# Attention plan on measured durations, weights on ScalarE's transfer queue, low parts in quarters, a reordered front

## The chip, the cores and the metric

One NeuronCore of a Trainium2 chip runs the program. The metric is the device time in microseconds (us) of one execution. Below, PE is TensorE, ACT is ScalarE, DVE is VectorE, POOL is GpSimd and SP is SyncE; "ACTq" and "SPq" are the places on ACT and SP where transfers are issued.

## What is computed

A hybrid encoder block in float32 on 512 tokens of 1024 channels, with 16 learned meta tokens in front (528 columns in all):

```python
u = rms_norm(h, pre_mix_gain);  proj = u @ w_in
qa, ka, va, qb, kb, vb, g = split(proj)
qa, ka, qb, kb = rope(...)                 # on each
o_swa  = windowed_gqa_sink_attention(qa, ka, va, sink)      # 16 q heads, 4 kv heads, blocks of 128
o_diff = rms_norm((softmax(q1 k1) - lam * softmax(q2 k2)) @ vb) * (1 - lambda_init)   # 8 heads
merged = sigmoid(g1) * (o_swa @ w_branch_swa) + sigmoid(g2) * (o_diff @ w_branch_diff)
h = h + rms_norm(merged @ w_out)
f = (silu(u2 @ w_gate) * (u2 @ w_up)) @ w_ffn_out;  h = h + rms_norm(f)     # u2 = rms_norm(h), 2816 wide
```

## The kernel before

Each float32 operand is split into a high part and a low part (`wh`, `wl`; `xh`, `xl`), and each product is three matmuls: high by high, high by low, low by high (`mm3`, lines 287 to 289). The weights come in tiles of 128 x 1024 (512 KB). For each one, `weights` (line 520) issues the transfer into `wr` (L527, on SP; three buffers), casts the high part on ACT (L529) and subtracts the low part on POOL for odd tiles and on DVE for even ones (L253). `products` (line 536) makes eight k-steps of `mm3` from one tile; each waits for all of `wh` and `wl`.

The program has four parts. In the **front**, 60 small matmuls on zeros (`warm`, L380) run first. Then the K projection (L447) takes its two weight tiles in parts of 2, 2 and 4 k-steps, the V projections follow (`pV`, then `pV2` by `v2(0)` and `v2(1)`), and between them the row sums of squares give the normalizing factors `rbc` (L491, L492). The order here is the order of the text.

The **attention plan** comes next. `Plan` holds a list of tasks with an engine, a cost, what they read and write, buffers with slots, and a priority. `Plan.run` walks through time: for each engine it finds the tasks that can start first and takes the one that is due first (for PE the priority itself, for the others the time at which it could start plus a slack by priority). Tasks with `port` never overlap each other. The engines then run in just this order; on the chip every wait is a semaphore, so a wrong cost changes the order and not the result. The tasks are: V for the windowed heads (`v_swa`), the rotated K (`rope_t`, L554 to L558, then transfers between partitions by `move`, L576), four groups of Q (`q_swa`), gates (`gate`), 16 windowed units (`s_swa`: scores `Sw` L715, exponentials, scaling on POOL L729; `t_swa`: transposes L764, products `O` L771), then per differential head `qk`, `vd`, `s_diff` (scores `Sd` L863, minimum L868, exponential L871, reciprocal L874, its product with -lam on DVE L881, combination L884) and `t_diff` (transposes L918, products `Od` L931 and L933, a sum of squares `mp` L945 and L946). `b1` and `gate2` are filler products. `lam_task` makes `nlam`, which is -lam. In `vd` a 16 x 128 copy `m.t[64:80]` runs on DVE (L843).

The **third part** starts behind the plan: for eight column tiles `bd_products` multiplies by `w_bd`. For the first two tiles the k-steps 0 to 6 are issued ahead of the k-step that needs the last head. `load_w` (L268) loads there; by its counter `nw`, loads 4 to 17 make three quarters of the low part on POOL. The **fourth part**, output projection and feed-forward, follows.

Of the kernel before, what the change touches and what calls it, by code (L numbers as in the profile page):

```python
# [109 lines left out]
class Task:  # L110
    def __init__(self, n, eng, cost, fn, prio, port, land):
        self.n, self.eng, self.cost, self.fn, self.prio, self.port, self.land = n, eng, cost, fn, prio, port, land
        self.deps, self.alloc, self.bufs, self.done, self.start = set(), [], [], None, None


class Plan:
# [59 lines left out]
    def run(self):  # L176
        free = self.free
        port = 0.0
        todo = {e: [k for k in self.tasks if k.eng == e] for e in free}
        self.idle = []  # L180
        while any(todo.values()):
            best = None
            for e, ks in todo.items():
                cand = []
                for k in ks:
                    t = 0.0
                    for d in k.deps:
# [9 lines left out]
                    for tag, n in need.items():  # L197
# [4 lines left out]
                        t = max(t, f[n - 1] + 0.07)  # L202
# [4 lines left out]
                    cand.append((max(t, free[e], port if k.port else 0.0), due, k))  # L207
# [30 lines left out]
def encoder(ctx, tc, I, out, dbg=None):  # L238
# [89 lines left out]
    nlam = const.tile([P, 1], F32, name="nlam")  # L328
    qsc = const.tile([P, 1], F32, name="qsc")
# [49 lines left out]
    for _ in range(60):  # L379
        pe.matmul(out=wps[:, 0:P], lhsT=warm, rhs=warm, start=True, stop=True)  # L380
# [20 lines left out]
    def w_part(w, n, k0, k1):  # L401
        if k0 == 0:
            w.extend([wp.tile([P, KT, P], F32, tag="wr", name="wr", bufs=RB),
                      wp.tile([P, KT, P], F32R, tag="wh", name="wh"), wp.tile([P, KT, P], F32R, tag="wl", name="wl")])
        ks = slice(k0, k1)
        sp.dma_start(out=w[0][:, ks], in_=I["w_in"][n].rearrange("p (k c) -> p k c", k=KT)[:, ks])
        split(w[1][:, ks], w[2][:, ks], w[0][:, ks])

    wA, wB = [], []
    for k in range(KT):  # L410
        x_load(k)
        x_split(k)
        for k0, k1 in {0: ((0, 2),), 1: ((2, 4),), 3: ((4, KT),)}.get(k, ()):
            w_part(wA, 0, k0, k1)
            w_part(wB, 1, k0, k1)
    wA, wB = wA[1:], wB[1:]
# [24 lines left out]
    for k in range(KT):  # L441
        todo = [(ps_, w[a][:, k, :], (xh, xl)[b][:, k, cs], k == 0 and a == b == 0, k == KT - 1 and a == 1)
                for hs, w in ((kA, wA), (kB, wB)) for ps_, cs in zip(hs, halves) for a, b in ((0, 0), (0, 1), (1, 0))]
        if k == 0:
            todo = [x for p in range(3) for x in todo[p::3]]
        for ps_, a, b, first, last in todo:
            pe.matmul(out=ps_, lhsT=a, rhs=b, start=first, stop=last)  # L447
# [42 lines left out]
    v2(1, range(KT))  # L490
# [9 lines left out]
    for c in range(2):  # L500
# [9 lines left out]
                   ta=2, tb=1, vt=1, rt=RT, ma=3), dict(PE=4.3, ACT=0.05, DVE=0.05, POOL=0.0, SP=0.0))  # L510
# [10 lines left out]
    def weights(src, dep=()):  # L521
# [5 lines left out]
        T("SP", 0.35, lambda: sp.dma_start(out=wr.t, in_=src.rearrange("p (k c) -> p k c", k=KT)),  # L527
          w=[wr], dep=dep, prio=pr_, land=3.6 if nfill[0] > 3 else 0.3)
        T("ACT", 1.05, lambda: act.copy(out=wh.t, in_=wr.t), r=[wr], w=[wh], prio=pr_)  # L529
        if nfill[0] % 2:  # L530
            T("POOL", 2.65, lambda: sub_hi(wl.t, wr.t, wh.t, pool), r=[wr, wh], w=[wl], prio=pr_, port=True)
        else:
            T("DVE", 1.23, lambda: sub_hi(wl.t, wr.t, wh.t), r=[wr, wh], w=[wl], prio=pr_, port=True)
        return wh, wl

    def products(w, x, xb, c0, c1, dep=()):
# [3 lines left out]
        for k in range(KT):  # L540
            T("PE", 3 * mm_t(c1 - c0),
              lambda k=k: mm3(pb.t[:, 0:c1 - c0], (wh.t[:, k, :], wl.t[:, k, :]),
                              (x[0][:, k, c0:c1], x[1][:, k, c0:c1]), k == 0, k == KT - 1),
              r=[wh, wl] + xb, w=[pb], dep=dep, prio=20 + nfill[0])
        return pb

    def rope_t(hl, pa, pb, c0, n, p0, o0, scale, more=False):
# [16 lines left out]
        T("DVE", 0.15 + 0.55 * m, lambda: half(ta, pa, 1), r=[pa, ROT], w=[ta], prio=3)  # L564
        T("DVE", 0.15 + 0.55 * m, lambda: half(tb, pb, 0), r=[pb, ROT], w=[tb], prio=3)
# [1044 lines left out]
```

## Time and profile before

| | |
|---|---|
| median of three runs | 949.84 us (948.51 to 950.56) |
| profiled execution | 949.22 us, span of its instructions 947.4 us |
| busy, share of the span | PE 98%, weight loads 88%, DVE 76%, ACT 55%, POOL 23% |
| transfers | 110.46 MB, 117 GB/s over the span |
| front | 0 to 31.3 us |
| attention plan | 31.3 us (first V transposes) to 510.0 us |
| the rest | 510.0 to 947.4 us |

A busy share counts a matmul from its start to its modelled end, and neighbours overlap, so 98% doesn't say that PE runs at its rate. What PE loses is seen in the distance from one matmul's start to the next.

### The profile page before, as it was taken

The page shows a single profiled execution, that of the slowest core. Times are in us where ns is not written, and L with a number is a line of the kernel's source. Part 1 is how long each engine was busy: PE and PEld are TensorE (multiplying, and loading weights), DVE is VectorE, ACT ScalarE, POOL GpSimd, SP SyncE. Part 2 cuts the span into 40 slices and gives each one's busy share as a digit, 9 for nine tenths or more (in the row PEclk, how much of TensorE's full clock was granted, in tenths as well). Part 3 has the DMA queues.
Part 4 walks back from the last instruction along what each step waited for, and adds up shares of the span by engine and source line. Part 5 has one row for each costly group of instructions (what it writes and reads, how often), then busy time and mean ns, then how long its engine had stood idle before and what let it go on. Part 6 is the DMA issues. An engine that isn't in the chain of part 4 may idle for free.

```text
span 947.4 us, 15653 instructions
## 1 busy us (share of the span) xinstructions
PE 931.6 (98%) x5871; PEld 834.1 (88%) x5871; DVE 716.2 (76%) x1234; ACT 525.8 (55%) x957; POOL 216.0 (23%) x228
## 2 busy tenths in 40 slices
PE   9999999999999999999999999999999999999996
PEld 9788879889898999999888888998999999988885
DVE  5738898999564759877773865886787887799975
ACT  7337766775644446667556443654555555565541
POOL 0544455543222433243211421300000000000000
PEclk9999999999999999999999999999999999999999
DMA  9483132251425144433532460364323333180122
GB/s 319 160 220 102 51 104 58 63 148 45 123 89 157 46 122 127 105 96 115 157 112 67 161 216 23 100 186 141 117 104 101 117 95 112 46 333 13 55 67 89
DMA packets 38011, 110.46 MB, mean 117 GB/s; under 512 B 6177, under 2 KB 7457, under 8 KB 37937
## 3 DMA queue, kind: packets, MB, share of 16 engines
q1 hardware_dynamic: 37792, 109.34, 38.1%
q8 instruction: 46, 0.75, 0.3%
q14 instruction: 29, 0.23, 0.1%
q10 hardware_dynamic: 144, 0.13, 0.0%
HBM read 88.09 MB, written 2.10 MB: 95 GB/s over the span
## 4 chain that ended last, share of the span: by engine, by line
PE 86%; DVE 5%; DMA 4%; ACT 2%; issue 1%; SPq 1%; DVEq 0%; ACTq 0%
PE pr L287 19%; PE pr L289 19%; PE pr L288 19%; PE Sd L863 3%; PE wk L288 2%; PE wk L287 2%; PE wk L289 2%; PE Sw L715 2%; PE O L771 2%; PE tr L918 2%; PE Od L931 2%; PE tr L764 2%; DMA wr<-in_w_in_dram 2%; PE tr L288 1%; PE tr L287 1%; PE tr L289 1%
## 5 line engine op out<-in xcount | busy, mean ns | idle before, releaser
L287 PE MATMUL pr<-xh,wh 128*128 128x264 f32 (+1 forms) x592 | 193.4, 327 | 0.0
L289 PE MATMUL pr<-xh,wl 128*128 128x264 f32 (+1 forms) x592 | 190.0, 321 | 0.6 <-POOL wl L253 0.6
L288 PE MATMUL pr<-xl,wh 128*128 128x264 f32 (+1 forms) x592 | 189.8, 321 | 0.0
L253 POOL TENSOR_TENSOR wl<-wr,wh 128x1024 fp32r<-128x1024 f32 (+2 forms) x42 | 99.5, 2372 | 145.2 <-ACT wh L529 82.5
L289 PEld LDWEIGHTS pr<-xh,wl 128*128 128x128 f32 x592 | 111.6, 189 | 9.6 <-POOL wl L253 1.3
L288 PEld LDWEIGHTS pr<-xl,wh 128*128 128x128 f32 x592 | 111.9, 189 | 7.4
L287 PEld LDWEIGHTS pr<-xh,wh 128*128 128x128 f32 x592 | 111.8, 189 | 7.4 <-issue 0.2
L529 ACT CAST wh<-wr 128x1024 fp32r<-128x1024 f32 x56 | 58.5, 1048 | 47.0 <-PE pr L288 34.6
L309 POOL TENSOR_TENSOR r3y<-r3v,mhalf 128x1 f32<-128x1 f32 x4 | 2.2, 549 | 326.1 <-DVE r3v L308 326.1
L253 DVE TENSOR_TENSOR wl<-wr,wh 128x1024 fp32r<-128x1024 f32 (+2 forms) x61 | 69.0, 1134 | 10.0 <-ACT wh L272 8.2
L287 PE MATMUL pr<-TM,sx 128*128 128x256 f32 x236 | 66.9, 283 | 0.2 <-ACT s L1393 0.2
L289 PE MATMUL pr<-TM,sx 128*128 128x256 f32 x236 | 66.8, 283 | 0.0
L288 PE MATMUL pr<-TM,sx 128*128 128x256 f32 x236 | 66.8, 283 | 0.0
L868 DVE TENSOR_REDUCE nm<-Sd 128x1 f32<-128x528 f32 x64 | 45.1, 705 | 20.8 <-PE Sd L863 19.9
L253 DVE TENSOR_TENSOR sx<-S,sx 128x1024 fp32r<-128x1024 f32 x34 | 41.6, 1224 | 24.9 <-PE pr L288 12.7
L289 PE MATMUL pr<-uh,wl 128*128 128x256 f32 (+1 forms) x188 | 55.0, 292 | 0.4 <-DVE wl L253 0.4
L287 PE MATMUL pr<-uh,wh 128*128 128x256 f32 (+1 forms) x188 | 55.0, 293 | 0.0
L288 PE MATMUL pr<-ul,wh 128*128 128x256 f32 (+1 forms) x188 | 54.9, 292 | 0.0
L566 POOL TENSOR_TENSOR ta<-ta,tb 128x528 f32<-128x528 f32 (+1 forms) x26 | 37.0, 1422 | 74.5 <-DVE tb L554 45.3
L871 ACT ACTIVATE pp<-Sd,nm 128x528 f32<-128x528 f32 x40 | 27.9, 699 | 39.2 <-DVE pa L884 22.6
L257 ACT CAST sx<-S 128x1024 fp32r<-128x1024 f32 x34 | 35.7, 1050 | 25.1 <-PE pr L289 8.2
L729 POOL TENSOR_SCALAR p<-p,rc 128x272 f32<-128x272 f32 (+1 forms) x64 | 35.9, 573 | 47.9 <-DVE rc L727 44.5
(528 smaller groups left out, 2673.9 us busy)
## 6 DMA issues: line engine op xcount, KB each, us to landing
wr<-in_w_in_dram SPq DMA_DIRECT2D x50, 512.0 KB, 4.1
wg<-in_w_fi_dram SPq DMA_DIRECT2D x17, 512.0 KB, 3.6
wu<-in_w_fi_dram SPq DMA_DIRECT2D x17, 512.0 KB, 3.5
wr<-in_w_fi_dram SPq DMA_DIRECT2D x16, 512.0 KB, 3.8
b<-in_w_fo_dram SPq DMA_DIRECT2D x16, 512.0 KB, 8.5
Kd<-hl SPq DMA_DIRECT2D x32, 132.0 KB, 2.4
Kd<-Kd SPq DMA_DIRECT2D x16, 264.0 KB, 3.7
Q<-hl SPq DMA_DIRECT2D x64, 64.0 KB, 2.8
```

Source lines behind the costliest of these rows:

```text
L253: (eng or dve).tensor_tensor(out=lo, in0=src, in1=hi.bitcast(F32), op=ALU.subtract)
L257: act.copy(out=hi, in_=src)
L287: pe.matmul(out=ps, lhsT=ah, rhs=bh, start=first, stop=False, **more)
L288: pe.matmul(out=ps, lhsT=ah, rhs=bl, start=False, stop=False, **more)
L289: pe.matmul(out=ps, lhsT=al, rhs=bh, start=False, stop=last, **more)
L529: T("ACT", 1.05, lambda: act.copy(out=wh.t, in_=wr.t), r=[wr], w=[wh], prio=pr_)
L566: T("POOL", 0.05 + 1.3 * m, lambda: pool.tensor_tensor(out=ta.t[:, :, 0:n], in0=ta.t[:, :, 0:n], in1=tb.t[:, :, 0:n], op=ALU.add), r=[tb], ...
L715: pe.matmul(out=Sw2[S.slot][:, 0:nk], lhsT=QS[g][hh].t[:, i * P:(i + 1) * P], rhs=KB[g].t[:, x, r0:r1], start=(x == 0), stop=(x == 1))
L729: T("POOL", 0.2 + 0.43 * c, lambda z=z: pool.tensor_scalar(out=pt.t[:, z, 0:nk], in0=pt.t[:, z, 0:nk], scalar1=rc.t[:, z:z + 1], scalar2=1 ...
L863: pe.matmul(out=S.t[:, s, 0:HALF], lhsT=Q[c].t[:, i * P:(i + 1) * P], rhs=K[c].t[:, x, s * HALF:(s + 1) * HALF], start=(x == 0), stop=(x = ...
L868: T("DVE", 0.71, lambda S=S, c=c, one=one: dve.tensor_reduce(out=nm.t[:, c, one], in_=S.t[:, :, 0:HALF], axis=AX.XY, op=ALU.min), r=[S], w ...
L871: T("ACT", 0.9, lambda S=S, c=c, one=one, p=p: act.activation(out=p().rearrange("p (a b) -> p a b", a=2), in_=S.t[:, :, 0:HALF], func=AF.E ...
```

## The change

- Front: the two K weight tiles are laid out by k-step, both tiles side by side (`w_k`), and come in four transfers of 256 KB between those of x; the K loop goes k by k over both. 41 warm-up matmuls instead of 60.
- The V product `v2(1)` moves from the front into the plan as eight tasks, and the rotation of K (`k_swa`) is entered behind both `v_swa` and waits for the V scaling (`VT`).
- From the fourth weight tile on, `weights` issues its transfer on ACT's queue; three stay on SP.
- Low parts on POOL are made in four instructions of two k-steps each, and a k-step waits for its own quarter only.
- The product with -lam: instead of DVE L881 behind the reciprocal, ACT multiplies the denominator by 1/nlam (`ilam`) ahead of it. The 16 x 128 copy of `vd` moves from DVE to ACT.
- The first 14 k-steps of `w_bd` become tasks of the plan, with the two loads.
- `Plan`: other costs for most tasks, engine-dependent gaps and delays (`OVER`, `DRAIN`, `lag`), a model of the two transfer queues by size (`kb`), every POOL task on the port, and `SHIFT`, 136 numbers that are added to the due times of single tasks. Two dependencies between heads are added (`ms`, `zs`).

The diff, cut to its core:

```diff
+    OVER = dict(PE=0.0, ACT=0.098, DVE=0.083, POOL=0.03, SP=0.0)
+    DRAIN = dict(PE=0.165, ACT=0.0, DVE=0.0, POOL=0.0, SP=0.0)
+    SHIFT = (
+        "12:50.00 34:2.24 35:2.80 71:11.00 119:17.00 170:4.71 307:-48.00 312:-37.00 316:-1.91 340:-0.48 "
...
-        k = Task(len(self.tasks), eng, cost, fn, prio, port, land)
+        k = Task(len(self.tasks), eng, cost, fn, prio, port or eng == "POOL", land, kb)
...
+                    due += self.shift.get(k.n, 0.0)
+                    cand.append((max(t, free[e], port + 0.02 * (holder == e) if k.port else 0.0), due, k))
...
+            if k.kb:
+                q = queue[k.eng] = max(t + 1.4, queue[k.eng]) + k.kb / (205.0 if k.eng == "SP" else 270.0)
+                k.done = q + (0.35 if k.eng == "SP" else 1.0)
...
-    for _ in range(60):
+    for _ in range(41):
         pe.matmul(out=wps[:, 0:P], lhsT=warm, rhs=warm, start=True, stop=True)
...
+    def k_weights(i):
+        if i % 2 == 0:
+            wK.append([wp.tile([P, 4, 2, P], dt, tag=t, name=t, bufs=RB) for t, dt in (("wr", F32), ("wh", F32R), ("wl", F32R))])
+        w = [t[:, 2 * (i % 2):2 * (i % 2) + 2] for t in wK[-1]]
+        sp.dma_start(out=w[0], in_=I["w_k"][i].rearrange("p (k a c) -> p k a c", k=2, a=2))
+        split(w[1], w[2], w[0])
+    for what in ("x0", "w0", "x1", "x2", "w1", "x3", "x4", "w2", "x5", "x6", "w3", "x7"):
...
-    v2(1, range(KT))
...
-                   ta=2, tb=1, vt=1, rt=RT, ma=3), dict(PE=4.3, ACT=0.05, DVE=0.05, POOL=0.0, SP=0.0))
+                   ta=2, tb=1, vt=1, rt=RT, ma=3), dict(POOL=0.0, PE=0.4, ACT=0.05, DVE=0.05, SP=0.0))
...
-        T("SP", 0.35, lambda: sp.dma_start(out=wr.t, in_=src.rearrange("p (k c) -> p k c", k=KT)),
-          w=[wr], dep=dep, prio=pr_, land=3.6 if nfill[0] > 3 else 0.3)
+        e, eng, kb = ("ACT", act, 512) if nfill[0] > 3 else ("SP", sp, 0)
+        T(e, 0.38, lambda: eng.dma_start(out=wr.t, in_=src.rearrange("p (k c) -> p k c", k=KT)), w=[wr], dep=dep,
+          prio=pr_, land=0.7, kb=kb)
...
-            T("POOL", 2.65, lambda: sub_hi(wl.t, wr.t, wh.t, pool), r=[wr, wh], w=[wl], prio=pr_, port=True)
+            for q in range(4):
+                ks = slice(2 * q, 2 * q + 2)
+                parts.append(T("POOL", 0.69, lambda ks=ks: sub_hi(wl.t[:, ks], wr.t[:, ks], wh.t[:, ks], pool), r=[wr, wh],
+                               keep=[wl], prio=pr_))
...
-              r=[wh, wl] + xb, w=[pb], dep=dep, prio=20 + nfill[0])
+              r=[wh] + xb, w=[pb], keep=[wl], dep=list(dep) + [wl.parts[k // 2]], prio=20 + nfill[0])
...
+    for k in range(KT):
+        T("PE", 0.367, lambda k=k: v2(1, [k]), r=W2, w=PV2[1:], prio=9)
...
+    def k_swa():
+            rope_t(hk, KR[0], KR[1], s * HALF, HALF, s * HALF, s * HALF, 1.0, more=(s == 0), dep=VT)
...
-        T("DVE", 0.22, lambda: dve.tensor_copy(out=m.t[64:80], in_=m.t[0:16]), r=[m], w=[m], prio=2)
+        T("ACT", 0.25, lambda: act.copy(out=m.t[64:80], in_=tm.t[0:NMETA, 0:P]), r=[tm], w=[m], prio=2)
...
+                if c:
+                    T("ACT", 0.2, lambda one=one: act.activation(out=den.t[:, 1, one], in_=den.t[:, 1, one], func=AF.Copy,
+                                                                 scale=ilam), w=pw, on=["lam"], prio=0)
...
-                    T("DVE", 0.16, lambda one=one: dve.tensor_tensor(out=rc.t[:, 1, one], in0=rc.t[:, 1, one], in1=nlam,
-                                                                    op=ALU.mult), on=[("r", h, c, i), "lam"],
...
-            hd["Av"].append(T("PE", 2 * mm_t(512), high, r=[ah, V], w=[O], prio=0))
+            hd["Av"].append(T("PE", 0.463, high, r=[ah, V], w=[O], dep=ms[-1:], prio=0))
...
-        T("ACT", 0.59, lambda: act.copy(out=ob.t, in_=O.t), r=[O], w=[ob], prio=0)
+        T("ACT", 0.59, lambda: act.copy(out=ob.t, in_=O.t), r=[O], w=[ob], dep=zs[-1:], prio=0)
...
+    for j in range(2):
+        wh, wl = weights(I["w_bd"][j], heads[7]["S"][4 + j:5 + j])
+        pb = bank("pr", 3, "pr")
+        for k in range(KT - 1):
+            T("PE", 0.694, lambda k=k, wh=wh, wl=wl, pb=pb: mm3(
+                pb.t, (wh.t[:, k, :], wl.t[:, k, :]), (dd[0][:, k, :], dd[1][:, k, :]), k == 0, False),
+              r=[wh, DD[k]], w=[pb], keep=[wl], dep=[wl.parts[k // 2]], prio=200 + j)
...
-    first = [(load_w(I["w_bd"][j]), pr_t()) for j in range(2)]
-    for b in first:
-        bd_products(b, range(KT - 1))
+    first = [((wh.t, wl.t), pb.t) for wh, wl, pb in first]
```

More of the change, by code (lines that the diff above doesn't have):

```diff
@@ L122, with lag @@
     SLACK = {-1: 0.0, 0: 0.0, 1: 0.4, 2: 1.5, 3: 2.0, 4: 3.0, 5: 6.0, 6: 8.0, 7: 15.0}
-    AFTER = dict(PE=0.22, ACT=0.07, DVE=0.07, POOL=0.12, SP=0.1)
+    OVER = dict(PE=0.0, ACT=0.098, DVE=0.083, POOL=0.03, SP=0.0)
+    DRAIN = dict(PE=0.165, ACT=0.0, DVE=0.0, POOL=0.0, SP=0.0)
+    SHIFT = (
[15 rows of a table added]
+    )
+    @staticmethod
+    def lag(a, b):
+        return (0.77 if a == "SP" else 0.27) if b == "PE" else 0.06 if b == "SP" else 0.092 if b == "POOL" and a in ("ACT", "DVE") else 0.036
     def __init__(self, tags, free):
         self.free = free
+        self.shift = {int(n): float(x) for n, x in (y.split(":") for y in self.SHIFT.split())}
         self.slots = {t: [0.0] * n for t, n in tags.items()}
@@ L177, in run @@
         free = self.free
-        port = 0.0
+        port, holder, queue = 0.0, None, dict(SP=0.0, ACT=0.0)
         todo = {e: [k for k in self.tasks if k.eng == e] for e in free}
@@ L190, in run @@
                             break
-                        t = max(t, d.done + (0.0 if d.eng == e else self.AFTER[d.eng]))
+                        t = max(t, d.start + d.cost if d.eng == e == "PE" else d.done + self.lag(d.eng, e))
                     if t is None:
@@ L225, in run @@
             k.start = t
-            free[k.eng] = t + k.cost
-            k.done = t + k.cost + k.land
+            free[k.eng] = t + max(0.06, k.cost - self.OVER[k.eng]) if k.eng != "PE" else t + k.cost
+            k.done = t + k.cost + k.land + self.DRAIN[k.eng]
+            if k.kb:
+                q = queue[k.eng] = max(t + 1.4, queue[k.eng]) + k.kb / (205.0 if k.eng == "SP" else 270.0)
+                k.done = q + (0.35 if k.eng == "SP" else 1.0)
             if k.port:
-                port = t + k.cost
+                port, holder = t + k.cost, k.eng
             k.fn()
@@ L233, in run @@
                 if not b.left and b.tag is not None:
-                    self.slots[b.tag][b.slot] = max(u.done + (0.0 if u.eng == "PE" else 0.0) for u in b.users)
+                    self.slots[b.tag][b.slot] = max(u.done for u in b.users)
         self.end = max(k.done for k in self.tasks)
@@ L399, in x_split @@
                                  in1=xh[:, k, :].bitcast(F32), op0=ALU.mult, op1=ALU.subtract)
[L401 to L416, printed above, removed]
+    wK = []
+    def k_weights(i):
[5 more added lines that the diff above has]
+    for what in ("x0", "w0", "x1", "x2", "w1", "x3", "x4", "w2", "x5", "x6", "w3", "x7"):
+        n = int(what[1])
+        if what[0] == "w":
+            k_weights(n)
+        else:
+            x_load(n)
+            x_split(n)
     wV = load_w(I["w_in"][2], dst=[atp.tile([P, KT, P], F32R, tag="p", name="wV", bufs=2) for _ in range(2)])
@@ L441, in encoder @@
     for k in range(KT):
[L442 to L447, printed above, removed]
+        w = [t[:, k % 4] for t in wK[k // 4][1:]]
+        for a, b in ((0, 0), (0, 1), (1, 0)):
+            for n, hs in enumerate((kA, kB)):
+                for ps_, cs in zip(hs, halves):
+                    pe.matmul(out=ps_, lhsT=w[a][:, n, :], rhs=(xh, xl)[b][:, k, cs], start=(k == a == b == 0),
+                              stop=(k == KT - 1 and a == 1))
     pV = [tr_t()[:, 0:HALF], tr_t()[:, 0:HALF]]
@@ L648, in encoder @@
     PV2 = [pl.held("pr", t) for t in pV2]
+    W2 = [pl.held(t, x) for t, x in zip(("wh", "wl"), wV2)]
+    for k in range(KT):
+        T("PE", 0.367, lambda k=k: v2(1, [k]), r=W2, w=PV2[1:], prio=9)
     for b in MK:
@@ L705, in s_swa @@
         sm = [buf() for _ in range(2)]
[L706 removed]
+        T("POOL", 0.2, lambda: pool.tensor_copy(out=pt.t[:, :, nk], in_=nsink[:, 4 * g:4 * g + 4]),
           w=[pt] + ph, prio=0)
@@ L901, in lam_task @@
         T("DVE", 0.16, lambda: dve.tensor_scalar(out=nlam, in0=nlam, scalar1=-LAMBDA_INIT, scalar2=None, op0=ALU.add),
-          w=[LS], sig="lam", prio=7, port=True)
-    lnx, dd, results, B1 = [], [], [], []
+          w=[LS], prio=7, port=True)
+        T("DVE", 0.16, lambda: dve.reciprocal(out=ilam, in_=nlam), w=[LS], sig="lam", prio=7)
+    lnx, dd, results, B1, DD, zs, ms = [], [], [], [], [], [], []
     def t_diff(h):
```

122 lines of the change are left out of this document (64 added, 58 removed), and 14 rows, old and new, of the table SHIFT.

## The prediction

> **What bounds the kernel now.** I read the page's head first, then the table of stretches, the groups of matmuls in the plan, the timeline for PE's rates, and last the waits and the chain around them.
>
> ```profile
> span 947.4 us, 15653 instructions
> ```
>
> The table by stretch (length, busy time of PE, weight loads, DVE, ACT, POOL with counts, then granted PE clock, transfer share, GB/s):
>
> ```profile
> 6.26:24.95 18.69, 18.09 (x149) 17.68 (x146) 12.11 (x21) 13.47 (x24) 1.20 (x1) 1.00 1.01 371
> 31.32:40.00 8.68, 6.74 (x28) 5.00 (x27) 7.90 (x11) 3.51 (x7) 7.42 (x5) 0.80 0.22 66
> 40.00:72.50 32.50, 32.03 (x139) 25.61 (x137) 14.05 (x19) 9.26 (x11) 11.96 (x8) 1.00 0.83 214
> 72.50:150.00 77.50, 77.14 (x395) 63.05 (x396) 67.40 (x193) 54.59 (x140) 34.31 (x57) 1.00 0.28 77
> 150.00:220.00 70.00, 68.95 (x456) 61.79 (x455) 64.96 (x167) 51.35 (x130) 36.52 (x54) 1.00 0.34 92
> 220.00:250.00 30.00, 29.27 (x192) 26.01 (x191) 23.18 (x43) 16.42 (x34) 8.61 (x5) 1.00 0.47 123
> 250.00:400.00 150.00, 149.89 (x1044) 139.26 (x1043) 102.59 (x191) 79.07 (x149) 45.85 (x33) 1.00 0.35 97
> 400.00:450.00 50.00, 49.03 (x366) 45.83 (x365) 38.60 (x74) 35.36 (x69) 19.97 (x16) 1.00 0.39 117
> 510.04:947.40 437.36, 428.99 (x2709) 389.01 (x2707) 340.81 (x435) 222.94 (x329) 33.10 (x25) 1.00 0.35 114
> ```
>
> PE is the bound everywhere; idle is length minus busy. In the plan it is 1.94 us in 31 to 40, then 0.47, 0.36, 1.05, 0.73, 0.11 and 0.97, with 0.20 in the stretch to 510 not shown: 3.9 from 40 on. The clock is below 1.00 in one stretch only. But busy hides lengthened matmuls, so I count the plan's PE work from its groups (first and last of 30 groups) and the distances of starts:
>
> ```profile
> L287 PE MATMUL pr<-xh,wh 128*128 128x264 f32 x384 | 111.2, 290 | 0.0
> L599 PE MATMUL tr<-ident,vr 128*128 128x128 f32 x2 | 0.7, 345 | 0.0
> ```
>
> ```profile
> 28.40 0.28 PE L287 MATMUL pr<-xh,wh 128*128 128x264 f32 x1
> 31.20 0.28 PE L289 MATMUL pr<-xh,wl 128*128 128x264 f32 x1
> 492.39 0.49 PE L918 MATMUL tr<-ident,pa 128*128 128x128 f32 x3
> 492.83 0.49 PE L918 MATMUL tr<-ident,pa 128*128 128x128 f32 x3
> 505.88 0.39 PE L287 MATMUL pr<-xh,wh 128*128 128x512 f32 x1
> 510.04 0.40 PE L287 MATMUL pr<-dh,wh 128*128 128x512 f32 x1
> ```
>
> By these, 264 columns take 2.80 us / 23 = 0.1217, four transposes 0.44 (0.11 each), 512 columns 4.16 / 18 = 0.2311. The groups hold 1408 matmuls of 264 columns (171.4 us), 984 of 512 (227.4), 386 transposes (42.5), and 64 each of 400 and 272 columns (scaled between: 0.181 and 0.125, 19.6). Sum 460.9. The stretch 31.32 to 510.04 lasts 478.7, so **17.8 us** of it isn't PE work at its rate. That, and what the front loses, is all the change can remove: the matmuls stay. Behind 510 the code is the same.
>
> **The stall at the plan's start.**
>
> ```profile
> 28.76 3.98 POOL L253 TENSOR_TENSOR wl<-wr,wh 128x1024 fp32r<-128x1024 f32 x1
> 30.53 2.77 DVE L554 TENSOR_TENSOR ta<-kraw,rot 128x528 f32<-128x528 f32 x1
> 35.14 0.33 DVE L628 SCALAR_TENSOR_TENSOR Vm<-tr,vec,Vm 128x128 fp32r<-128x128 f32 x1
> 35.62 0.69 PE L607 MATMUL tr<-ident,VT 128*128 128x128 f32 x3 [1.65 <-DVE Vm L628]
> ```
>
> ```profile
> 32.43:35.84 3.41, 1.47 (x7) 0.92 (x7) 3.16 (x7) 0.87 (x4) 2.15 (x3) 1.00 0.47 156
> 35.84:39.25 3.41, 3.41 (x12) 2.72 (x11) 3.32 (x4) 1.25 (x3) 3.41 (x3) 0.50 0.00 0
> ```
>
> The K rotation on DVE (2.77 us, as it waits out POOL's 3.98 us subtraction) runs ahead of the V split, and PE waits 1.65 us for that split. Then the clock is 0.50 for 3.41 us, which costs half of it, 1.7. With 0.3 us of waiting for POOL's low part the stretch loses 1.94 + 1.7 = 3.6 of the 17.8; 14.2 lie between 40 and 510.
>
> **The change part by part.**
>
> *Front: 19 fewer warm-ups, K weights by k-step.*
>
> ```profile
> 0.97 5.48 PE L380 MATMUL wps<-warm 128*128 128x128 bf16 x60 [0.97 <-DVE warm L377]
> 6.26 0.61 PE L447 MATMUL pr<-xh,wh 128*128 128x264 f32 x3
> 4.59 0.95 ACT L257 CAST wh<-wr 128x256 fp32r<-128x256 f32 x2 [0.21 <-DMA wr<-in_w_in_dram]
> 16.90 1.23 DVE L253 TENSOR_TENSOR wV<-wr,wV 128x1024 fp32r<-128x1024 f32 x1 [1.52 <-ACT wV L272]
> 25.91 0.68 DVE L253 TENSOR_TENSOR wl<-wr,wh 128x512 fp32r<-128x512 f32 x1
> ```
>
> ```profile
> 5.20:6.20 1.00, 1.00 (x22) 1.00 (x20) 0.74 (x2) 0.73 (x2) 0.00 (x0) 1.00 0.80 244
> ```
>
> The last warm-ups come at some 18 per us (22 touched, 4 begun earlier), so 19 fewer free at most 1.05 us; the first weights are cast by 5.54, so K can begin 0.5 to 1 earlier. What follows is set by transfers, which fill 1.01 of 6.26 to 24.95, and the bytes are the same: the V weights' low part is done at 18.13 (K ended at 19.1, so at most 1.0 is to be had there), and the second low half of `wV2` at 26.59. I take 0.6 at the plan's start (0 to 1.05). `v2(1)` as eight tasks of the plan: the same matmuls, and cover for the V path.
>
> *K rotation behind V, in the plan.* This takes the DVE work out of the way of the split and the stall goes, with its half clock. Late next is the first Q product's low part; it now needs one POOL quarter (a quarter of 2.5 us, row below), which lies beside `v2(1)` (8 x 0.365 us). K's transfers start later, with some 30 us of Q and gate products before the first scores as cover; without it they would cost what they are late. I take 3.3 of 3.6 (0 to 3.6).
>
> The Trainium skill (TensorE: Matmul & The Clock Gate, section Why this matters for your kernels) lets the clock drop only behind idle gaps over about 3 us. This trace differs: PE was busy 1.47 of 3.41 us and the next 3.41 ran at half clock. By the page the half clock would stay and 1.7 less be gained; the measurement decides.
>
> *Low parts in quarters, the -lam product and the copy moved to ACT.*
>
> ```profile
> 224.26 2.40 POOL L253 TENSOR_TENSOR wl<-wr,wh 128x1024 fp32r<-128x1024 f32 x1 [1.21 <-ACT wh L529]
> 224.60 2.14 DVE L843 CAST Vdm<-Vdm 16x128 fp32r<-16x128 f32 x1
> 326.52 1.02 DVE L881 TENSOR_TENSOR rc<-rc,nlam 128x1 f32<-128x1 f32 x1
> 230.62 0.77 PE L863 MATMUL Sd<-Kd,Qd 128*128 128x264 f32 x4 [0.73 <-ACT pp L871]
> L253 POOL TENSOR_TENSOR wl<-wr,wh 128x1024 fp32r<-128x1024 f32 (+1 forms) x29 | 73.0, 2517 | 103.2 <-ACT wh L529 82.5 <-ACT wh L272 20.7
> L881 DVE TENSOR_TENSOR rc<-rc,nlam 128x1 f32<-128x1 f32 x32 | 7.1, 223 | 0.7
> ```
>
> The tiny copy took 2.14 us: it ended with POOL's subtraction (226.66). All of DVE's chain stood behind it, and PE idled 0.73 at 230. Both small operations leave DVE (32 x 0.223 = 7.1 us, and 8 copies), and a POOL instruction can now hold DVE for some 0.65 us, not 2.4. POOL has slack for 87 more instructions (36.5 of 70 us busy at its fullest). ACT's chain per score block grows by one small instruction, where DVE loses one of like size: nothing net.
>
> *Other costs, shifts, first `w_bd` steps in the plan.* These only reorder. What of the 14.2 us goes can't be read from a row; bounds are 0 and 14.2, and an order can lose too. The nearest row is the kernel's own best stretch: 250 to 400 idles 0.11 in 150 us with the same kinds of task. At that rate the 3.9 us of idle become 0.35: 3.5 gained. The 10.3 us of lengthened matmuls partly follow late releases (a weight load that couldn't run ahead) and partly every group of transposes; I give a third, 3.5. Together 7.0. The stretch 450 to 510 has little to give, so the `w_bd` steps bring nothing. The POOL share of `load_w` shifts by two loads into the feed-forward: nothing.
>
> *Weights on ACT's queue.*
>
> ```profile
> 943.78 0.37 ACTq L1523 DMA_DIRECT2D out_dram<-f  x1
> SPq L527 <- POOL wl L253: 87.9, 14, 15.5
> ```
>
> One issue on ACT takes 0.37 us; 58 tiles less three make 55 x 0.37 = 20 us over 470. The fullest stretch, 150 to 220, has ACT busy 51.35 of 70; some 8 issues add 3. So ACT has room, and SP's moves no longer stand behind weight issues that wait for POOL (87.9 us in 14 waits). Against this, a weight issue that comes early now holds all of ACT. I take 0.5 us lost (0 to the case below).
>
> Sum: -0.6 - 3.3 - 7.0 + 0.5 = **-10.4 us**, from the profiled 949.22 to 938.8; the median stands 0.62 above the profiled run, so 939.4. With all bounds at their best: 1.05 + 3.6 + 14.2 = 18.9 off, 931.
>
> **Rivals.**
> 1. *Stalls move, none goes between 40 and 510.* For: DVE is busy 67.4 of 77.5 and 65.0 of 70 us in the windowed units, which lose no DVE work, and durations vary (0.22 to 2.14 for one copy). Against: 250 to 400. Gain 0.6 + 3.3 - 0.5 = 3.4: 946.4.
> 2. *The second queue does nothing for the moves.* The Trainium skill (DMA: Bandwidth & Descriptors, section Issuing engines are not separate DMA queues) says transfers of all engines interleave on the same 16 and only issue time is saved. As a mechanism here: transfers fill 0.83 of 40 to 72.5, so Q still lands late and the 1.8 us of idle from there to 220 stay with their share of lengthening: 3.3 less, 942.7.
> 3. *Slower: ACT is held at its own queue.* The buffer that an issue wants is freed by POOL or DVE; on SP such waits averaged 87.9 / 14 = 6.3 us and held nobody else. On ACT the exponentials and casts behind it wait, and PE after them. The gain is used up when the 55 issues hold PE 10.9 / 55 = 0.2 us each; at 0.3 they cost 16.5, so 16.5 - 10.9 = 5.6 over: 955. Against: ACT is only 73% busy where it is fullest.
> 4. *No change*: a smaller hold (0.2) eats the gain: 949.8.
>
> **How the numbers follow.** Forecast (934 to 944.5) with its part-way versions 0.50, rival 2 0.12, rival 1 0.17, rival 4 0.08, rival 3 0.13. A run of this kernel tells 0.2% (1.9 us) from nothing, about the spread of the three runs. Faster: 0.50 + 0.12 + 0.17 = 0.79; within 0.2%: 0.08; slower: 0.13. The range 931 to 950 leaves out rival 3 and a little more.
>
> **What would show it.** Right: no wait of PE for L628, clock 1.00 from the plan's start, plan's end near 499.6 on the trace's time; no DVE instruction of 2 us beside a POOL quarter; idle per stretch under 0.5. Wrong: ACT's queue waiting at weight issues with exponentials behind, PE waiting for ACT, or a new idle of PE between warm-up and K that brings the half clock back.

## The result and the profile after

The changed kernel takes 956.18 us (median of 5 runs, 953.32 to 961.29) against 949.84 for the one before on the same chip: 1.0063 of it, 95% interval 1.0038 to 1.0089. It is slower; the forecast was 939.4. The profiled execution took 961.04, near the top of its spread.

```profile
span 959.2 us, 15645 instructions
```

The stretches of the plan again (same columns as before the change: length, busy PE, weight loads, DVE, ACT, POOL, granted clock, transfer share, GB/s), then four of one length of 3.41 or twice that:

```profile
31.32:40.00 8.68, 8.68 (x48) 7.35 (x47) 7.88 (x11) 4.37 (x7) 4.89 (x6) 1.00 0.38 118
40.00:72.50 32.50, 31.03 (x134) 24.86 (x133) 13.72 (x19) 8.85 (x12) 18.61 (x21) 1.00 0.78 194
72.50:150.00 77.50, 76.95 (x391) 62.39 (x390) 64.70 (x181) 53.44 (x133) 36.30 (x65) 1.00 0.28 81
150.00:220.00 70.00, 67.98 (x462) 61.32 (x461) 66.13 (x177) 52.10 (x134) 37.10 (x63) 1.00 0.35 92
220.00:250.00 30.00, 28.27 (x185) 24.96 (x184) 20.86 (x41) 16.25 (x39) 6.92 (x9) 1.00 0.40 107
250.00:400.00 150.00, 144.00 (x960) 132.41 (x959) 94.47 (x155) 82.25 (x163) 57.51 (x63) 0.97 0.33 89
400.00:450.00 50.00, 47.09 (x358) 44.59 (x358) 39.49 (x70) 30.61 (x68) 16.41 (x21) 1.00 0.46 128
304.19:311.02 6.83, 6.09 (x18) 5.21 (x19) 0.96 (x3) 0.79 (x2) 0.70 (x1) 0.50 0.00 1
348.56:351.97 3.41, 3.41 (x18) 3.41 (x17) 1.41 (x4) 1.97 (x6) 0.71 (x1) 0.50 0.00 0
3.82:7.23 3.41, 1.59 (x21) 1.42 (x20) 1.43 (x2) 1.57 (x3) 0.52 (x3) 1.00 0.95 290
7.23:10.64 3.41, 3.41 (x17) 3.41 (x17) 2.88 (x6) 3.35 (x6) 0.00 (x0) 0.50 1.03 388
```

The stall at the plan's start is gone: PE is busy 8.68 of 8.68 us from 31.32, at full clock. But from 40 to 450 its idle time has grown from 3.69 us (0.47, 0.36, 1.05, 0.73, 0.11, 0.97) to 14.68 (1.47, 0.55, 2.02, 1.73, 6.00, 2.91), by 11.0. The stretch that was best before, 250 to 400, is now the worst, and its clock is 0.97: behind two of the waits PE ran 9.5 us (6.09 + 3.41) at half clock, another 4.75 lost. A third half clock stands behind the warm-ups. The waits of PE (total, times, longest):

```profile
PE Sd L900 <- DMA Qd<-hl: 11.2, 6, 3.7
PE pr L476 <- ACT wh L286: 1.8, 1, 1.8
PE pr L316 <- DVE ta L590: 1.5, 1, 1.5
```

11.2 us in six waits are scores of the differential heads that stand in PE's order before their Q has come. The longest, in the timeline (SP issues the moves, ACT the weight loads; idle time in brackets; rows left out are marked):

```profile
289.90 1.08 SPq L612 DMA_DIRECT2D Qd<-hl  x1
289.99 0.35 ACTq L557 DMA_DIRECT2D wr<-in_w_in_dram  x1
...
293.03 0.33 ACTq L557 DMA_DIRECT2D wr<-in_w_in_dram  x1
...
299.16 0.50 SPq L612 DMA_DIRECT2D Kd<-Kd  x1
299.69 1.90 SPq L612 DMA_DIRECT2D Qd<-hl  x3
299.98 0.34 ACTq L557 DMA_DIRECT2D wr<-in_w_bs_dram  x1
304.93 1.25 PE L900 MATMUL Sd<-Kd,Qd 128*128 128x264 f32 x4 [3.65 <-DMA Qd<-hl]
```

Three loads of 512 KB go out among the moves of this head; the last three Q moves, issued from 299.69, land at 303.14, 304.88 and 305.18. The medians from issue to landing, before and after:

```profile
Kd<-hl SPq DMA_DIRECT2D x32, 132.0 KB, 2.4
Qd<-hl SPq DMA_DIRECT2D x64, 64.0 KB, 2.1
```

```profile
wr<-in_w_in_dram ACTq DMA_DIRECT2D x45, 512.0 KB, 4.2
Kd<-hl SPq DMA_DIRECT2D x32, 132.0 KB, 2.6
Qd<-hl SPq DMA_DIRECT2D x64, 64.0 KB, 3.3
```

Sorted by whether a weight load is in flight beside it (a load counted from 0.5 us behind its issue, a move from 1.0 us), a Qd move of the changed kernel takes a median of 2.37 us without one (29 of them) or 4.73 with one (35). The kernel before: 2.04 (33) and 3.65 (31). The changed plan counts 1.4 + 64/205 + 0.35 = 2.06 us to the landing and 0.77 from there to PE (`lag`), so it allows 2.83 from issue to score. The plan before allowed 3.4 (0.6 of issue, 2.7 of landing, 0.1). For a move of K before the K-to-K move behind it (`Kd<-Kd`) the allowance went from 3.3 to 2.45.

The moves also leave late. `Kd<-Kd` waits on SP until `Kd<-hl` has landed, and the Q moves behind it in SP's order wait with it. SP's waits there, before and after:

```profile
SPq L576 <- DMA Kd<-hl: 1.4, 1, 1.4
```

```profile
SPq L612 <- DMA Kd<-hl: 14.2, 8, 3.2
```

When PE had nothing else to do, the Q move that it waited for had been issued only 0.2, 0.9, 1.7, 2.9, 4.1 and 4.4 us before, in the six waits: in three of them even a move of 2.06 us would have been late.

### The profile page after: what moved, and what is told of

The parts are those of the page before. It is cut to its first block, busy times and chain, and to the rows that moved or that the text cites. A ratio compares the mean times of both kernels' runs of the same rounds, so it can differ in the third digit from the quotient of the medians.

```text
span 959.2 us, 15645 instructions
## 1 busy us (share of the span) xinstructions
PE 933.2 (97%) x5852; PEld 836.0 (87%) x5852; DVE 712.5 (74%) x1192; ACT 534.1 (56%) x995; POOL 239.6 (25%) x316
## 4 chain that ended last, share of the span: by engine, by line
PE 81%; DMA 7%; DVE 5%; SPq 3%; ACT 2%; issue 1%; DVEq 0%; ACTq 0%
PE pr L316 18%; PE pr L317 18%; PE pr L318 18%; PE Sd L900 4%; DMA Kd<-hl 3%; SPq L612 3%; DMA Qd<-hl 3%; PE wk L317 2%; PE wk L316 2%; PE wk L318 2%; PE tr L316 2%; PE tr L318 2%; PE tr L317 2%; PE Sw L752 1%; PE O L808 1%
## 5 line engine op out<-in xcount | busy, mean ns | idle before, releaser
L282 POOL TENSOR_TENSOR wl<-wr,wh 128x256 fp32r<-128x256 f32 (+1 forms) x130 | 120.6, 951 | 139.5 <-ACT wh L559 88.1
L559 ACT CAST wh<-wr 128x1024 fp32r<-128x1024 f32 x58 | 60.7, 1047 | 30.3 <-PE pr L317 30.0
L900 PE MATMUL Sd<-Kd,Qd 128*128 128x264 f32 x256 | 45.8, 302 | 12.1 <-DMA Qd<-hl 11.2
L900 PEld LDWEIGHTS Sd<-Kd,Qd 128*128 128x128 f32 x256 | 37.5, 195 | 18.1 <-DMA Qd<-hl 10.2
L766 POOL TENSOR_SCALAR p<-p,rc 128x272 f32<-128x272 f32 (+1 forms) x64 | 38.5, 615 | 49.5 <-DVE rc L764 49.5
```

The lines of the kernel that those rows point to most:

```text
L282: (eng or dve).tensor_tensor(out=lo, in0=src, in1=hi.bitcast(F32), op=ALU.subtract)
L766: T("POOL", 0.22 + 0.41 * c, lambda z=z: pool.tensor_scalar(out=pt.t[:, z, 0:nk], in0=pt.t[:, z, 0:nk], scalar1=rc.t[:, z:z + 1], scalar2=1.0,
L900: pe.matmul(out=S.t[:, s, 0:HALF], lhsT=Q[c].t[:, i * P:(i + 1) * P], rhs=K[c].t[:, x, s * HALF:(s + 1) * HALF], start=(x == 0), stop=(x = ...
```

## Experiments

**T1**: transfers of both queues share the engines that carry them. The plan takes them for independent and a move for 2.06 us; beside a load it takes 4.7, and PE's in-order queue holds scores ahead of it. **T2**: the order with its 136 shifts is poor whatever the moves do. **T3**: ACT is held by its own weight issues (my third rival). **Theory F**: 41 warm-ups are too few. All ratios are to the kernel before on the same chip.

| run | what it is | median us | ratio (95% interval) |
|---|---|---|---|
| `e1_warm60` | changed kernel, 60 warm-ups | 955.48 | 1.0038 (1.0015 to 1.0060) |
| `e7_half` | changed kernel, loads of 256 KB | 942.72 | 0.9917 (0.9890 to 0.9945) |
| `e10_quarter` | changed kernel, loads of 128 KB | 942.09 | 0.9907 (0.9879 to 0.9935) |
| `e8_sameq` | changed order, loads on SP's queue | 964.02 | 1.0139 (1.0090 to 1.0187) |
| `e6b_same_plan_act` | order before, loads on ACT's queue | 948.88 | 0.9984 (0.9969 to 0.9998) |
| `e6_before_act` | the same, and the plan before knows it | 966.36 | 1.0176 (1.0141 to 1.0211) |
| `e2_land` | moves 2.3 us later in the changed plan | 969.37 | 1.0193 (1.0159 to 1.0227) |
| `e3_noshift` | no shifts | 952.55 | 1.0029 (1.0002 to 1.0055) |
| `e5_share_ns` | no shifts, one shared row of transfers in the plan | 955.40 | 1.0046 (1.0024 to 1.0068) |
| `e4_oneq_ns` | no shifts, loads on SP's queue, in the plan too | 950.43 | 0.9988 (0.9975 to 1.0001) |
| `e11_oneq_order` | one queue, own list of shifts | 949.18 | 0.9988 (0.9972 to 1.0004) |
| `e12_twoq_order` | two queues, own list of shifts | 955.20 | 1.0055 (1.0037 to 1.0073) |
| `e14_twoq_cover` | two queues, own list with cover behind the last head | 946.84 | 0.9967 (0.9955 to 0.9979) |
| `e16_oneq_cover` | one queue, own list with that cover | 948.59 | 0.9975 (0.9960 to 0.9989) |
| `e17_oneq_warm60` | the same, 60 warm-ups | 947.62 | 0.9971 (0.9958 to 0.9984) |

**Fewer bytes, same order.** The casts and subtractions read the part that came once more for the rest, so these two kernels compute with other weights; only their times are of use.

```diff
-        T(e, 0.38, lambda: eng.dma_start(out=wr.t, in_=src...), w=[wr], ...)
+        T(e, 0.38, lambda: eng.dma_start(out=wr.t[:, 0:4], in_=src...[:, 0:4]), w=[wr], ...)   # 0:2 in the second run
```

> The changed kernel with the same plan and order, in which each of the 55 weight loads on ACT's queue brings only its first 256 KB (the upper half of its rows is made from the lower half, so the products are of other weights; number and shape of instructions on PE, ACT, DVE and POOL stay). Theory T1: moves are held up half as long, so beside a load they land in about 3.4 us instead of 4.8, PE's idle at the differential scores falls from 11.2 us to 4 to 6, the half-clock stretches go, and the time is 944 to 950. Theory T2 (order) and T3 (ACT held by issues, whose number stays): no change, 953 to 959.

> As the run with half the bytes, but each of the 55 weight loads on ACT's queue brings only its first 128 KB, from which the other three quarters of its rows are made (products of other weights; plan, order, number and shape of instructions stay). With 512 KB the kernel takes 956, with 256 KB 943. Theory T1 (what is lost is late moves beside loads): the moves land in 2.0 to 3.0 us, no wait of PE for moves is left, and the time is at or a little under that with 256 KB: 939 to 943. If the order had more to give than the moves take away, under 938. If half the bytes helped through something else (the casts' inputs coming earlier), the step is as large again: about 936.

With 256 KB, the stretches from 220 on (first fence) and the transfers (second); then the same with 128 KB:

```profile
220.00:250.00 30.00, 30.00 (x189) 26.46 (x188) 21.10 (x42) 17.79 (x42) 7.31 (x10) 1.00 0.30 81
250.00:400.00 150.00, 149.85 (x1049) 139.07 (x1048) 104.59 (x172) 86.07 (x170) 59.06 (x63) 1.00 0.28 74
```

```profile
wr<-in_w_in_dram ACTq DMA_DIRECT2D x45, 256.0 KB, 2.9
Qd<-hl SPq DMA_DIRECT2D x64, 64.0 KB, 2.7
```

```profile
250.00:400.00 150.00, 150.00 (x1052) 139.58 (x1051) 104.76 (x172) 86.52 (x172) 59.14 (x64) 1.00 0.24 59
```

No wait of PE for a move is left, no half clock in the plan, and 250 to 400 idles 0.15 and 0.00 instead of 6.00. A Qd move beside a load takes 3.05 us (256 KB) and 2.48 (128 KB; without a load 2.67 there), SP's waits for `Kd<-hl` are 3.6 us with 256 KB instead of 14.2, and PE's order is the same. By the ratios, half of the bytes bring 14 us, the next quarter 1, which isn't told apart from nothing: the lateness costs only from where it outruns the slack of the order. T2 and T3 can't explain this: neither the order nor the number of issues changed. If casts with earlier inputs had brought it, the second run was expected to gain as much again, to 936; it didn't. It also says what the whole change is worth if no move comes late: 8 us under the kernel before, 3.6 of them the stall at the plan's start. The kernel before wasn't run with fewer bytes, but in its trace PE waits for a transfer only once, 0.5 us, so it had little to gain by them.

**The queue alone, from both sides.** In the first run the changed kernel's loads go back to SP's queue at the same place in the plan; in the second the loads of the kernel before go to ACT's queue and its plan isn't told; in the third it is told.

```diff
-        T(e, 0.38, lambda: eng.dma_start(out=wr.t, ...            # e8: after
+        T(e, 0.38, lambda: sp.dma_start(out=wr.t, ...
-        T("SP", 0.35, lambda: sp.dma_start(out=wr.t, ...          # e6b: before
+        T("SP", 0.35, lambda: (act if nfill[0] > 3 else sp).dma_start(out=wr.t, ...
-        T("SP", 0.35, lambda: sp.dma_start(out=wr.t, ...          # e6: before
+        T("ACT" if nfill[0] > 3 else "SP", 0.35, lambda: (act if nfill[0] > 3 else sp).dma_start(out=wr.t, ...
```

> The changed kernel with the same plan and order of tasks, but the 55 weight loads are issued on SP's queue, at the place in its order where the plan has them on ACT. Theory T3 (ACT held by its issues): ACT is free of 55 issues of 0.37 us and the time falls, to 945 to 952. Theory T1: moves now stand behind the load on the one queue instead of beside it, so they come no earlier; idle of PE at the differential scores is 10 to 20 us and the time 955 to 968. If the two queues are independent of each other, as the plan assumes, moves come later by the whole load and the time is 965 or more.

> The kernel before with its plan and order untouched, in which the 55 weight loads behind the first three are issued on ACT's queue, at the place in its order where the plan has them on SP. So nothing moves but the queue. Theory T1: moves beside a load land in 4 to 5 us instead of 3.65 and use up the 3.4 us that this plan allows, so PE idles 2 to 6 us more at scores: 951 to 957. Theory T3 (ACT is held by the issues, whose cost this plan doesn't know on ACT): PE's waits for ACT's exponentials and casts grow, 955 to 970, without longer waits for moves. If the second queue helps: under 948.

> The kernel before with one edit: the 55 weight loads behind the first three are issued on ACT's queue (its plan knows it, with the landing times it had). Its plan still gives a move 2.7 us of landing behind 0.6 of issue, 4.0 for K to K. Theory T1: moves beside a load land in about 4.7 us instead of 3.65, so PE's idle at the differential scores grows by 2 to 6 us over the kernel before, and the time is 951 to 957. Theory T3 (ACT held by its issues): PE waits for ACT instead, over 955. If the second queue helps the moves, as I forecast: 947 to 949.

Waits of PE, on one queue with the changed order, then in the kernel before with its loads on ACT's queue:

```profile
PE Sd L900 <- DMA Qd<-hl: 8.6, 4, 3.4
PE Sd L900 <- issue: 2.8, 1, 2.8
PE Sw L752 <- DMA Q<-hl: 1.9, 1, 1.9
```

```profile
PE Sd L864 <- DMA Qd<-hl: 0.5, 1, 0.5
```

So one queue doesn't save the changed order (964, as T1 expected), and two queues don't hurt the order before (0.9984), though there too a Qd move beside a load takes 4.35 us instead of 3.65: its plan had left 3.4, and products between. My expectation of 951 to 957 from T1 was a miss: the new order loses on either queue and the order before on neither, so the loss comes with the order, which leaves late moves less room. How much of that is the shorter allowance, and how much the order of the other tasks, these runs don't separate. T3 falls as well: 55 issues on ACT cost that kernel nothing. The third run, over 955 as its expectation had it for T3, lost 14 us by the medians, but PE's waits for ACT at the differential scores are 2.6 us in all and those for Qd 1.6:

```profile
200.00:250.00 50.00, 43.03 (x281) 35.85 (x280) 46.41 (x111) 33.46 (x83) 22.11 (x26) 1.00 0.45 127
```

```profile
ACT wh L530 <- PE pr L288: 60.4, 25, 11.3
```

PE idles 7 us between 200 and 250, in 18 pieces, with the loads' issues and casts elsewhere in ACT's order; at the casts (second fence) ACT itself waits 60.4 us, against 34.6 in the kernel before and 42.3 with its order kept. As the same loads in the old order cost nothing, it is the order; what in it was not followed.

**Telling the plan.** One constant for every move; the shifts emptied; one shared row of transfers in the model; the loads back on SP in the model too.

```diff
-                k.done = q + (0.35 if k.eng == "SP" else 1.0)                                        # e2
+                k.done = q + (2.65 if k.eng == "SP" else 1.0)
-    SHIFT = ( ... )                                                                                  # e3, e4, e5
+    SHIFT = ""
-                q = queue[k.eng] = max(t + 1.4, queue[k.eng]) + k.kb / (205.0 if k.eng == "SP" else 270.0)   # e5
+                q = queue["SP"] = queue["ACT"] = max(t + 1.4, queue["SP"]) + k.kb / 205.0
-        e, eng, kb = ("ACT", act, 512) if nfill[0] > 3 else ("SP", sp, 0)                              # e4
+        e, eng, kb = "SP", sp, 512 if nfill[0] > 3 else 0
```

> The changed kernel with one constant of its plan's model changed: a move is taken to land 2.65 us behind its bytes instead of 0.35, so about 4.4 us from issue, which is what the trace shows beside a weight load (median 4.7 to 4.8). Only the order of instructions changes; both queues, the quarters, the front and the 136 shifts stay. Theory T1 (PE's in-order queue holds scores ahead of moves that land later than the plan believes, because weight loads on the other queue share the transfer engines): the idle of PE at the differential scores falls from 11.2 us to under 4, at most one half-clock stretch is left in the plan, and the time is 942 to 950. Theory T2 (the order with its 136 shifts is poor whatever the moves do): 953 to 962. Theory T3 (ACT is held by its own weight issues): no change, 954 to 958.

> The changed kernel with the list of 136 shifted due times emptied; model, queues, quarters and front stay. Theory T2 (the shifts make a poor order): without them PE's idle at the differential scores halves and the time is 946 to 951. Theory T1 (moves land later than the model says, beside the weight loads): scores are still put ahead of late moves, PE idles 8 to 15 us at the scores, half-clock stretches stay, and the time is 955 to 966.

> The changed kernel without the shifts, and with one shared row of transfers in the plan's model in place of two independent queues: a weight load's 512 KB hold up the moves behind them, both at 205 KB per us. Second queue, quarters and front stay. Theory T1: the plan now puts scores where the moves have landed; PE's idle at the differential scores falls under 4 us and the time is 942 to 951, faster than without the shifts and with independent queues. Theory T2 or T3: no better than that other run.

> The changed kernel without the shifts and with the weight loads back on SP's queue, in the model too, where they hold up the moves behind them. The rest of the change (quarters, new front, measured durations, small operations moved to ACT) stays. Theory T1: with a queue that the model describes, PE's idle at the differential scores is under 5 us and the stall at the plan's start stays away, so the time is 943 to 951. If the rest of the change is what loses: over 953.

The largest wait for scores in each, in this order:

```profile
PE Sd L884 <- DMA Qd<-hl: 3.9, 3, 2.3
```

```profile
PE Sd L884 <- ACT pp L892: 2.5, 2, 2.2
```

```profile
PE Sd L884 <- ACT pp L892: 0.3, 1, 0.3
```

```profile
PE Sd L900 <- ACT pp L908: 7.5, 7, 2.6
```

(`e3_noshift`, `e5_share_ns`, `e4_oneq_ns`, and last `e2_land`.) Where the model lengthens or shares the moves, PE no longer waits for a Q move. That much is T1. But the time didn't follow: `e2_land`, expected at 942 to 950, took 969 and lost more elsewhere (PE idles 20.2 us from 40 to 450). Its plan leaves 1.4 + 0.31 + 2.65 + 0.77 = 5.13 us from issue to score for every move, more than the 4.73 beside a load. I take it that a pessimistic landing for every move delays the chain of each head, and that the 136 shifts were numbers for another order; the two weren't tried apart. So a larger allowance for all moves, the obvious cure, isn't one here. Emptied, the shifts bring 3 us by the ratios (1.0063 to 1.0029, overlapping intervals), between what T1 and T2 expected: it may be that part of T2 holds, as waits for Q fell from 11.2 to 3.9. `e5_share_ns` missed its 942 to 951: its waits only moved, to exponentials and casts. `e4_oneq_ns` was inside its range, no better than the kernel before.

**Orders made for shared transfers.** One or two queues, the shared row in the model, a load's landing counted 1.0 us behind its bytes on either queue, and new lists of some 700 due times, chosen by random trials on landings up to 1.6 us late.

```diff
-    SHIFT = ( ... 136 entries ... )
+    SHIFT = ( ... 719 to 785 entries ... )
-                q = queue[k.eng] = max(t + 1.4, queue[k.eng]) + k.kb / (205.0 if k.eng == "SP" else 270.0)
-                k.done = q + (0.35 if k.eng == "SP" else 1.0)
+                q = queue["SP"] = queue["ACT"] = max(t + 1.4, queue["SP"]) + k.kb / 205.0       # two queues
+                q = queue[k.eng] = max(t + 1.4, queue[k.eng]) + k.kb / 205.0                    # one queue, loads on SP
+                k.done = q + (1.0 if k.kb == 512 else 0.35)
```

> The changed kernel (front, quarters, small operations on ACT) with the weight loads back on SP's queue, a plan whose model has one shared row of transfers (loads and moves, 205 KB per us), and a list of shifts of its own: 783 due times, chosen by random trials on a model in which moves land up to 1.6 us late, loads up to 1.2 us, and operations of ACT, DVE and POOL take up to 6% longer. Theory T1 (the order has some 8 us to give when it is made for the landings that come): no wait of PE for a move over 1 us, no half-clock stretch in the plan, 938 to 944. If only fewer bytes in flight give that, and no order can: as without shifts on one queue, 948 to 952.

> The same with the loads left on ACT's queue as in the change, the shared row in the model and a list of 755 shifts chosen in the same way for that. Theory T1: the second queue itself costs nothing once the model knows the shared transfers, 938 to 945, against 956 of the change and 955 with the shared row without shifts. Theory T3 (ACT held by its issues is what loses): waits of PE for ACT stay at 3 us or more and the time is over 948.

Both missed, and have one loss in common. PE's longest wait with one queue, and ACT's rows behind the last sum of squares (`mp`, at 506.50):

```profile
PE pr L380 <- ACT dh L1070: 5.0, 1, 5.0
```

```profile
510.37 5.01 ACT L1165 ACTIVATE z<-z,hb 128x512 f32<-128x512 f32 x8
515.28 0.62 ACT L1058 ACTIVATE z<-y 128x512 f32<-128x512 f32 x1
518.17 0.62 ACT L1070 CAST dh<-ob 128x512 fp32r<-128x512 f32 x1 [2.27 <-DVE ob L1063]
```

The new lists had pulled the first `w_bd` steps ahead of the last head, whose chain of normalization on ACT (with eight activations of the gates in between) then stood uncovered; two half-clock stretches followed. My objective counted the plan alone. That explains the miss with one queue (8.4 us there); with two, 955.2 less the 7.2 lost there would still be over its range. With 13.5 us of products kept behind that sum, a first list for one queue (681 due times: `e13_oneq_cover`, and `e15_oneq_warm60` with 60 warm-ups) has no time: its order ends in a deadlock, and which tasks block each other wasn't followed. So a list of due times can do worse than a poor order, though the account of the plan says that a wrong cost changes the order alone. Three runs with other lists:

> The same for two queues (loads on ACT's queue, shared row in the model, 785 due times of its own, same condition). The run before it lost 7.2 us in the same place. Theory T1: 955.2 - 7.2 = 948; 944 to 949, so the second queue is no gain over one. Theory T3 (ACT held by its issues): waits of PE for ACT elsewhere, over 951.

> The changed kernel with the loads back on SP's queue, the shared row of transfers in the plan's model and a list of 719 shifts of its own, chosen under the condition that 13.5 us of products are left for PE behind the last head's sum of squares. The same without that condition took 949.2, and lost 8.4 us there. Theory T1: the order recovers what the late moves take: 939 to 944, at or below the two-queue order's 946.84. If orders only move the waits: 946 to 951.

> The same with 60 warm-up matmuls in place of 41. Theory F (41 are too few where the first weights come late): no half clock at K's start in any run, 0 to 1.7 us less than the same with 41, and a smaller spread. If 60 delay K: 0.3 to 0.6 us more.

```profile
220.00:250.00 30.00, 30.00 (x202) 27.19 (x201) 22.70 (x41) 18.58 (x40) 13.96 (x16) 1.00 0.50 142
250.00:400.00 150.00, 149.58 (x1042) 139.03 (x1041) 103.54 (x173) 86.30 (x175) 50.02 (x56) 1.00 0.37 97
400.00:450.00 50.00, 50.00 (x373) 47.12 (x372) 39.37 (x71) 36.22 (x77) 24.89 (x24) 1.00 0.41 114
```

With two queues (`e14_twoq_cover`, these rows) the plan idles 0.42 us from 220 to 450 with all 512 KB of each load, and the kernel beats both others: 946.84, 0.33% under the one before. As T1 foretold, the second queue costs nothing once the order allows for it. Its list, its condition and its model differ from those of the change together; which of them brings the gain wasn't tried apart. One queue is as fast (0.9975, its interval overlaps) but missed its 939 to 944 and fell where orders only move the waits: it idles 1.6 us from 72.5 to 150 and 2.0 to 220, in small waits (two queues: 1.7 and 2.2), and one stretch there runs at half clock. So an order made for later landings comes out three us under the kernel before, where the runs with fewer bytes came out eight under it. Whether the rest is to be had stays open.

**Warm-ups.**

```diff
-    for _ in range(41):
+    for _ in range(60):
```

> The changed kernel with the 60 warm-up matmuls of before in place of 41, nothing else. In the trace of the changed kernel PE idles 4.78 to 6.59 and the stretch from 7.23 runs at half clock. Theory F (the front lost by its fewer warm-ups): 19 warm-ups of 0.055 us fill the idle to about 5.8, no half clock behind K's start, K begins at 6.6 as before, and the time falls by 1.7 us, from 956.2 to about 954.5. If the front is of no account: within 0.5 us of 956.2.

```profile
3.82:7.23 3.41, 3.41 (x41) 3.41 (x39) 2.00 (x3) 2.29 (x4) 0.30 (x2) 1.00 1.00 349
7.23:10.64 3.41, 3.41 (x30) 3.41 (x30) 3.30 (x6) 3.31 (x6) 0.00 (x0) 1.00 1.03 376
```

With 60 the half clock at K's start is gone from the trace. In the times it isn't told apart: 1.0038 against 1.0063, overlapping intervals, and 0.9971 against 0.9975 for the one-queue order. With 41 it depends on when the first weights come: K began at 5.87 to 7.17 us in the traces, and not every wait brought the half clock (1.61 us of idle in `e14_twoq_cover` didn't).

## Why the prediction was wrong

- *Stall at the plan's start, -3.3*: right. All 3.6 went, with the half clock.
- *Front, -0.6 (0 to -1.05)*: the sign was wrong in the profiled run of the change. I let K begin when the first weights had been cast before; the first load is now 256 KB and its cast ends near 6.5, so PE idled 1.81 us, and the half clock that I had named as what could go wrong came back. The last V product started 0.8 later (25.63 for 24.83). But the half clock isn't all of it: in the nine traces of the changed kernel's variants with loads on ACT's queue that product starts at 24.55 to 25.63, in the five with all loads on SP's queue at 23.66 to 24.23, which is 0.6 to 1.2 earlier than before, about as forecast. In the changed kernel the first plan load on ACT's queue goes out at 15.63, while transfers still fill the front; I take it that this is where the gain went.
- *Low parts in quarters, -lam product and copy off DVE*: as predicted as far as the trace shows; a POOL quarter takes 0.74 us as a median, and in the plan no tiny DVE operation stands behind POOL for 2 us any more.
- *Reorder and shifts, -7.0 (0 to -14.2)*: the step that failed, in size and in sign. Even with loads of 128 KB, idle from 40 to 450 isn't under that of before (4.57 against 3.69). There the first product with `w_bd` starts 5.6 us earlier than before (504.46 for 510.04), of which the stall is 3.6, so the plan's other losses fell by about 2 us, not 7.0. With full loads they rose by 16 (the same product at 522.90, with 0.8 lost in the front). I bounded an order's loss at nothing, though I wrote that an order can lose. The row that would have told was in the trace of before: Qd 2.1 as a median, but 3.65 beside a load, while the diff cuts the allowance from a move's issue to its score from 3.4 to 2.83 us, that between the moves of K from 3.3 to 2.45, and puts 55 loads on a queue of their own. I read the new costs as measured ones and never held them against the transfers. I also named it a gain that SP's moves no longer stand behind weight issues; now they stand behind their own K moves (14.2 us).
- *Weights on ACT's queue, +0.5*: too dear for ACT (0.9984 in the unchanged order). Rival 3 named 955, which is close by luck, for a reason that didn't occur.
- *Rival 2, the Trainium skill's rule* (DMA: Bandwidth & Descriptors, Issuing engines are not separate DMA queues: transfers from all engines interleave on the same 16): the trace agrees, and goes further than my rival. I took it to mean that the moves come no earlier; beside a load they come 1.1 us later than beside one before (4.73 for 3.65; 0.7 where the queue alone changed, 4.35). I take it that bytes which used to wait behind a move in one queue now go beside it; no run shows that step by itself.

Together for the profiled run: 11.0 us of new idle from 40 to 450 and 0.9 behind, 4.75 of half clock, 0.8 of front, less 3.6 of the stall, make 13.8; the first product with `w_bd` starts 12.9 later (522.90 for 510.04), so about 1 us of lengthened matmuls may have gone.

## What to carry to other kernels

A plan with fixed costs is only as good as its dearest optimism: before trusting a new cost, hold it against the rows of the trace under load, for transfers above all, beside a load and without. Slack in front of an in-order queue looks like waste in a trace without waits; taken away, each late transfer becomes a wait, delays what stands behind it in its own queue, and the clock may charge it twice. One larger constant for all transfers didn't give the time back here (969). An order chosen on a model needs what follows it in the objective too, or the loss moves behind the model's end.

## What the hardware showed

Beside a 512 KB load on another queue, a 64 KB move between partitions went from medians of 2.0 to 2.6 us to 3.9 to 4.8 in the runs here (beside 256 KB from 2.59 to 3.05; beside 128 KB no longer, 2.48 against 2.67 without). Beside a load on its own queue it took 3.1 to 3.9. And the clock: in the changed kernel's run, counted in stretches of 3.41 us from 3.82 on, it fell to half behind those in which PE was busy 1.59, 1.20 and 0.49 us, and not behind those with 1.69, 1.94 and 2.33:

```profile
241.80:245.22 3.42, 1.69 (x9) 1.30 (x9) 1.27 (x2) 0.00 (x0) 0.00 (x0) 1.00 0.27 61
300.78:304.19 3.41, 0.49 (x3) 0.07 (x1) 0.00 (x0) 0.00 (x0) 0.00 (x0) 1.00 0.91 252
345.15:348.56 3.41, 1.20 (x10) 1.21 (x11) 0.43 (x1) 0.00 (x0) 2.71 (x4) 1.00 0.53 115
```

So a wait of 1.8 us can cost 3.5 and one of 1.7 only itself. PE's busy time in such a stretch doesn't settle it: the clock stayed up behind 1.72 (`e7_half`) and 1.80 (`e14_twoq_cover`), but fell behind 1.75 (`e6b_same_plan_act`), and in `e16_oneq_cover` behind 1.93, after three waits of which the longest was 0.58 us:

```profile
199.10:202.51 3.41, 1.93 (x13) 1.27 (x12) 3.27 (x12) 3.36 (x9) 2.08 (x4) 1.00 0.00 0
202.51:205.92 3.41, 3.41 (x13) 2.64 (x12) 2.56 (x7) 2.95 (x8) 2.92 (x7) 0.50 0.01 2
```

What else counts stays open. Such drops would explain why runs of the changed kernel spread over 8 us (their mean clocks go from 0.991 to 0.996), which wasn't tested by itself.
